# The first block of a hybrid decoder layer: x loaded by columns, ten k tiles multiplied unscaled and scaled on the way out of PSUM

## The chip, the cores and the metric

The kernel runs on one core of one Trainium2 chip. The metric is the device time of one execution in microseconds (us). The core's engines work beside each other and wait for one another through semaphores: TensorE (PE: matmuls and transposes; PEld: its weight loads), VectorE (DVE), ScalarE (ACT), GpSimd (POOL) and SyncE (SP), which here issues most of the DMAs. Each engine works through its own queue in the order in which the program left it.

## The reference, cut to what matters

One layer of two token mixers over 512 tokens of width 2048. Everything starts with an RMS norm and one wide projection:

```python
def _rmsnorm(x, w=None):
    xf = x.astype(jnp.float32)
    y = xf * lax.rsqrt(jnp.mean(xf * xf, axis=-1, keepdims=True) + NORM_EPS)
    return y if w is None else y * w.astype(jnp.float32)
...
    u = _rmsnorm(h, norm_w)
    proj = jnp.matmul(u, w_in.astype(jnp.float32))
    (ml_q, ml_k, ml_v, ml_o, ml_z, ml_i, ml_f,
     dn_qkv, dn_z, dn_b, dn_a, gate_a, gate_b) = jnp.split(proj, idx, axis=-1)
```

So u is x times a factor per token (the reciprocal root of its mean square) times a weight per column. The factor depends on all 2048 columns of a token, but it can be applied before the product with `w_in` or after it. The rest (the two mixers, the output projection, the gates, a final norm) isn't touched by the change.

## The kernel before

The kernel keeps u transposed: 16 **k tiles** of 128 columns by 512 tokens. Since a single f32r product isn't exact enough, u and every weight are split into a rounded part and a remainder (`uh`, `ul`; `wh`, `wl`), and one product becomes three matmuls: `uh` by `wh`, `ul` by `wh`, `uh` by `wl`. ScalarE makes the rounded part (`split_hi`, line 140), VectorE the remainder (`split_lo`, line 143). Weights come as tiles of two k tiles by 256 columns (`wr`, 256 KB; `load_raw`, line 172); four are in flight, and four splits of each kind.

The stage that the change touches is the start. SP issues x as eight half megabytes, two per chunk of 128 tokens (line 270). For each chunk ScalarE squares one half of the columns and VectorE the other (lines 297 and 299), the sums become the factor `rs` (lines 301 to 304, the power on GpSimd), and both engines scale the chunk in place (`scale_x`, lines 290 and 292). Then `make_u` turns each k tile: four transposes into a PSUM bank (`put`, line 313), ScalarE writes `uh` with the norm's column weight `normc` (line 314), VectorE `ul` (line 315). A tile needs all four chunks, so the first transposes wait for the factors.

The first block of the projection (`proj_cm` with `first_block` as its hook) multiplies k tile by k tile: two banks `pj` of 128 output columns each, 96 products in all. Ahead of the products of a pair, `first_block` turns tiles two further on, and from tile 8 it adds the **gate products** (lines 324 and 325): the 48 gate columns of `w_in`, kept as `wgp`, into the bank `pgr`. In the end `pgr` is copied to `gr0` and the two `pj` banks go out to memory with a scale (`spill`). The second block follows at once, over tiles 0 to 15; after its first six products TensorE turns `gr0` into the bank `pgt` (line 401), where the gate computation begins.

TensorE's order is written out by hand (`manual_schedule` for PE). The other engines' order comes from a scheduler with its own time estimates, nudged by `issue_after` and priorities. PSUM has eight banks: three `pj`, three `wk` (transposes, gates), two `o`.

## Time and profile before

| | us |
|---|---|
| median of three runs | 2155.34 (2155.28 to 2156.47) |
| the profiled execution, its own time | 2153.58 |
| its span, first to last instruction | 2151.8 |
| TensorE busy in the span | 2122.0 |
| VectorE busy | 1709.4 |
| ScalarE busy | 1042.1 |
| GpSimd busy | 431.0 |

The granted clock of TensorE is 0.999 throughout. A row of the timeline reads: start in us, how long, engine, line, operation, what is written and read (without buffer numbers), shapes, how many; in brackets the idle time of the engine before it and what ended it. A row for several instructions (x2, x8) spans from the first start to the last end. Lines in groups give the count, the busy time and the mean of one.

### The profile page before, as it was taken

How to read it: one execution, taken by the hardware profiler on the slowest of the kernel's cores; microseconds unless marked ns; L12 is line 12 of the kernel's file. 1: busy time of each engine (PE TensorE's matmuls, PEld its weight loads, DVE VectorE, ACT ScalarE, POOL GpSimd, SP SyncE). 2: the span in 40 equal slices, each digit the busy share in tenths (PEclk: the TensorE clock that was granted, in tenths of full speed). 3: DMA queues.
4: the chain of work that ended last, by engine and by line, in shares of the span. 5: the costliest groups of instructions: out<-in, count | busy, mean ns of one | idle time of the engine just before them, and what ended most of it. 6: DMA issues, size and time to landing. Idle time of an engine off the chain costs nothing. (4 is left out here: it accounts for less than half of the span.)

```text
span 2151.8 us, 31880 instructions
## 1 busy us (share of the span) xinstructions
PE 2122.0 (99%) x10544; PEld 1759.9 (82%) x10544; DVE 1709.4 (79%) x2973; ACT 1042.1 (48%) x1994; POOL 431.0 (20%) x651
## 2 busy tenths in 40 slices
PE   6999999999999999999999999999999999999998
PEld 5888888888888888888888888888888888887886
DVE  5888888788888778777756887887887878559887
ACT  5444444445444444444445545546455464345345
POOL 0000000000004000000012335334233263233211
PEclk9999999999999999999999999999999999999999
DMA  5456676667677767776767777677686677778895
GB/s 162 117 192 191 212 214 196 220 202 228 203 228 243 247 194 224 236 232 194 257 199 175 187 180 187 163 180 189 180 219 172 167 184 213 197 230 281 237 299 230
DMA packets 447143, 444.20 MB, mean 206 GB/s; under 512 B 197121, under 2 KB 303842, under 8 KB 446850
## 3 DMA queue, kind: packets, MB, share of 16 engines
q1 hardware_dynamic: 377618, 337.22, 54.5%
q0 software_dynamic: 24752, 72.90, 10.9%
q10 hardware_dynamic: 44608, 32.06, 4.7%
q8 instruction: 82, 1.34, 0.3%
q14 instruction: 83, 0.68, 0.1%
HBM read 348.66 MB, written 97.58 MB: 207 GB/s over the span
## 5 line engine op out<-in xcount | busy, mean ns | idle before, releaser
L140 ACT CAST wh<-wr 128x512 fp32r<-128x512 f32 (+1 forms) x522 | 373.9, 717 | 445.4 <-PE pj L258 239.2
L143 DVE TENSOR_TENSOR wl<-wr,wh 128x512 fp32r<-128x512 f32 (+1 forms) x522 | 438.3, 840 | 175.7 <-ACT wh L140 171.4
L257 PE MATMUL pj<-uh,wh 128*128 128x512 f32 x896 | 376.2, 420 | 0.0
L259 PE MATMUL pj<-uh,wl 128*128 128x512 f32 x896 | 351.1, 392 | 0.0
L258 PE MATMUL pj<-ul,wh 128*128 128x512 f32 x896 | 350.6, 391 | 0.0
L579 PE MATMUL ps<-wl,uh 128*128 128x512 f32 x752 | 292.6, 389 | 0.0
L578 PE MATMUL ps<-wh,uh 128*128 128x512 f32 x752 | 292.6, 389 | 0.0
L580 PE MATMUL ps<-wh,ul 128*128 128x512 f32 x752 | 292.6, 389 | 0.0
L140 ACT CAST wh<-t 128x1024 fp32r<-128x1024 f32 x120 | 126.4, 1053 | 294.0 <-PE ps L580 187.2
L578 PE MATMUL ps<-wh,suh 128*128 128x512 f32 x624 | 242.9, 389 | 0.0
L579 PE MATMUL ps<-wl,suh 128*128 128x512 f32 x624 | 242.8, 389 | 0.0
L580 PE MATMUL ps<-wh,sul 128*128 128x512 f32 x624 | 242.7, 389 | 0.0
L533 POOL DMA_DIRECT2D t_d<-ts x104 | 56.6, 544 | 922.3 <-DVE ts L520 854.1
L140 ACT CAST wh<-ts 128x512 fp32r<-128x512 f32 x240 | 148.3, 618 | 184.0 <-DVE ts L538 158.4
L143 DVE TENSOR_TENSOR wl<-t,wh 128x1024 fp32r<-128x1024 f32 x120 | 146.8, 1223 | 80.3 <-ACT wh L140 79.8
L259 PEld LDWEIGHTS pj<-uh,wl 128*128 128x128 f32 x896 | 168.4, 188 | 37.4
L257 PEld LDWEIGHTS pj<-uh,wh 128*128 128x128 f32 x896 | 169.3, 189 | 30.0
L258 PEld LDWEIGHTS pj<-ul,wh 128*128 128x128 f32 x896 | 169.4, 189 | 28.2
L143 DVE TENSOR_TENSOR wl<-ts,wh 128x512 fp32r<-128x512 f32 x240 | 164.3, 685 | 32.0 <-ACT wh L140 30.5
L580 PEld LDWEIGHTS ps<-wh,ul 128*128 128x128 f32 x752 | 141.2, 188 | 29.5
L579 PEld LDWEIGHTS ps<-wl,uh 128*128 128x128 f32 x752 | 141.2, 188 | 29.5 <-DVE wl L143 0.2
L578 PEld LDWEIGHTS ps<-wh,uh 128*128 128x128 f32 x752 | 141.2, 188 | 29.2
(334 smaller groups left out, 3760.7 us busy)
## 6 DMA issues: line engine op xcount, KB each, us to landing
wr<-in_w_in_dram SPq DMA_DIRECT2D x744, 256.0 KB, 3.6
wr<-in_w_out_dram SPq DMA_DIRECT2D x138, 256.0 KB, 4.9
t_d<-ts POOLq DMA_DIRECT2D x104, 256.0 KB, 3.7
wr<-t_d SPq DMA_DIRECT2D x104, 256.0 KB, 3.9
xt<-in_x_dram SPq DMA_DIRECT2D x8, 512.0 KB, 6.3
tg_d<-X ACTq DMA_DIRECT2D x16, 256.0 KB, 6.4
tg_d<-to ACTq DMA_DIRECT2D x16, 256.0 KB, 4.7
v<-v_d SPq DMA_DIRECT2D x8, 512.0 KB, 5.8
```

Of the source, the lines that this page charges most:

```text
L140: newest["A"] = A.copy(hi, src).ins
L143: newest["V"] = V.tensor_tensor(out=lo, in0=src, in1=hi.bitcast(F32), op=ALU.subtract).ins
L257: T.matmul(ps[j], hi[:, k, wsl], uh[:, kt, :], start=(kt == 0), stop=False)
L258: T.matmul(ps[j], hi[:, k, wsl], ul[:, kt, :], start=False, stop=False)
L259: T.matmul(ps[j], lo[:, k, wsl], uh[:, kt, :], start=False, stop=(kt == KT - 1))
L533: queue.dma_start(t2_d[b % 2, i], ts[:, 0, :])
L578: T.matmul(ps[t], ah, hi, start=(g == "A" and i == 0), stop=False, skip_group_check=True)
L579: T.matmul(ps[t], ah, lo, start=False, stop=False, skip_group_check=True)
L580: T.matmul(ps[t], al, hi, start=False, stop=(i == KH - 1), skip_group_check=True)
```

## The change

It takes apart the order "all factors first, then u". In the words of the code:

- x is one tile `xt` of four chunks by 2048 columns, loaded in five pieces by columns (256, 256, 512, 256, 768), the norm's weights ahead of them and four weight tiles between them.
- k tiles 0 to 9 (`KU = 10`) are turned and split **unscaled** (with `normc` alone). From tile 4 on, ScalarE first writes the whole value into columns of `xt` that are done with, and the split is made from there (`split_u`).
- The squares for the factors are spread over steps 0 to 7 (`square`, a step is six products), the sums come at step 7 (`token_factors`).
- Tiles 10 to 15 are scaled by `rs` ahead of their transposes (`scale_x`), as before.
- Products of tiles 0 to 9 stay in banks of their own (`rawp`, and `rawg` for the gates); tiles 10 to 15 go into other banks. `factor_row` and `turn_row` make `rrow`, the factor along the free axis on all partitions, by four matmuls of a matrix of ones with diagonals of `rs`. On copying out, the raw banks are multiplied by `rrow` and the other banks are added.
- Later blocks want scaled tiles: `rescale` and `rescaled` multiply tiles 0 to 9 by `rrow`, two at a time, and split them anew. The second block takes its k tiles in the order 10 to 15, 0 to 9 (`KS`).
- ScalarE and VectorE keep the written order in this stage (`manual_schedule` for both).

```diff
-GLAG = 8
+KU = 10
...
+    KS = {q: list(range(0, KT, KP)) for q in QK}
+    KS[QK[1]] = list(range(KU, KT, KP)) + list(range(0, KU, KP))
+    plan = [("i", (ML_Q, ML_K)[a] + b * NB, k) for a, b in QK for k in KS[a, b]]
...
+    load_norms(p0, psw)
+    xt = p0.tile([P, NC, D], F32, tag="x", name="xt")
+    XC = [0, 256, 512, 1024, 1280, D]
+    for n in range(len(XC) - 1):
+        o = slice(XC[n], XC[n + 1])
+        with behind("S") if n else ExitStack():
+            newest["S"] = nc.sync.dma_start(xt[:, :, o], xv[:, :, o]).ins
+        if n in (0, 1, 3, 4):
+            with behind("S"):
+                load_raw()
...
+    def turn_row(diag):
+        pr = psw.tile([P, S], F32, tag="wk", name="prow")
+        for c in range(NC):
+            T.matmul(pr[:, c * P:(c + 1) * P], ones, diag[:, c, :], start=True, stop=True)
+        A.copy(rrow, pr)
...
+    def split_u(kt, pt):
+        hi, lo = uh[:, kt, :], ul[:, kt, :]
+        if kt < 4 or kt >= KU:
+            A.activation(hi, pt, AF.Copy, scale=normc[:, kt:kt + 1])
+            V.scalar_tensor_tensor(out=lo, in0=pt, scalar=normc[:, kt:kt + 1], in1=hi.bitcast(F32), op0=ALU.mult, op1=ALU.subtract)
+        else:
+            f = whole(kt - 4, 1)[:, 0]
+            A.activation(f, pt.rearrange("p (c t) -> p c t", t=P), AF.Copy, scale=normc[:, kt:kt + 1])
+            split_hi(hi.rearrange("p (c t) -> p c t", t=P), f)
+            split_lo(lo.rearrange("p (c t) -> p c t", t=P), f, hi.rearrange("p (c t) -> p c t", t=P))
+
+    def rescale(p):
+        k = slice(KP * p, KP * (p + 1))
+        hi, lo, rr = (by_chunk(t) for t in (uh[:, k, :], ul[:, k, :], rrow.unsqueeze(1).to_broadcast([P, KP, S])))
+        if p < 2:
+            f = uf[p] = by_chunk(p0.tile([P, KP, S], F32, tag="uf", name="uf", bufs=2))
+            V.tensor_tensor(out=f, in0=hi.bitcast(F32), in1=lo.bitcast(F32), op=ALU.add)
+        else:
+            f = uf[p] = whole(KP * p - 4, KP)
+        V.tensor_tensor(out=f, in0=f, in1=rr, op=ALU.mult)
+        split_hi(hi, f)
...
+    SPLITS = {1: 1, 3: 2, 5: 3, 7: 4, 9: 5, 11: 6, 12: 7, 13: 8, 14: 9, 15: 10}
+
+    def hook(n):
+        if n in SPLITS:
+            split_next()
...
+        if n == 7:
+            square(A, 2, 2)
+            square(V, 2, 3)
+            token_factors()
+        if n == 8:
+            split_hi(wgh, wg)
+            split_lo(wgl, wg, wgh)
+            for kt in range(4):
+                gate_products(kt)
+            scale_x(KU, KU + 2)
+            gps["diag"] = factor_row()
+        if n == 9:
+            for kt in range(4, KU):
+                gate_products(kt)
+        if n == 10:
+            turn_row(gps["diag"])
+        if n == 13:
+            turn_taps(*taps, psw)
+        if n + 2 < KT:
+            split_u(n + 2, turn_x(n + 2))
...
+        if 10 <= n < 15:
+            rescale(n - 10)
+            if n > 10:
+                rescaled(n - 11)
+            if n == 10:
+                V.tensor_tensor(out=gr0, in0=rawg[0:112, :], in1=rrow[0:112, :], op=ALU.mult)
+            if n in (11, 12):
+                V.scalar_tensor_tensor(out=qk0[n - 11], in0=rawp[n - 11], scalar=QS, in1=rrow, op0=ALU.mult, op1=ALU.mult)
+        if n == 15:
+            rescaled(4)
...
+    with tc.manual_schedule(engines={mybir.EngineType.Activation, mybir.EngineType.DVE}):
+        pts = [turn_x(kt) for kt in range(2)]
+        split_u(0, pts[0])
+        split_next()
+        split_u(1, pts[1])
+        for j, p in enumerate(first_block()):
+            V.scalar_tensor_tensor(out=qk0[j], in0=p, scalar=QS, in1=qk0[j], op0=ALU.mult, op1=ALU.add)
+            nc.scalar.dma_start(qk_d[j], qk0[j])
+        V.tensor_tensor(out=gr0, in0=gr0, in1=gps["p"][0:112, :], op=ALU.add)
...
-    ps = proj_cm(ML_Q, before=first_block)
-    for kt in range(KT - GLAG, KT):
-        gate_products(kt)
-    gr0 = wp.tile([112, S], F32, tag="tg", name="gr0", bufs=3)
-    A.copy(gr0, pgr[0:112, :])
-    spill(ps, 0, float(P) ** -0.5)
```

How this moves the queues is seen at two places. The first is VectorE at the end of the first block, up to the copy of the gate transposes (`grow<-pgt`). Before, the last steps of the block stood there so:

```order
L143 TENSOR_TENSOR wl<-wr,wh 128x512
L315 SCALAR_TENSOR_TENSOR ul<-put,normc,uh 128x512 x2
L132 TENSOR_SCALAR convc<-pprt 128x192
L133 TENSOR_SCALAR normc<-pprt 128x16
L134 TENSOR_SCALAR normc<-pprt 128x1
L143 TENSOR_TENSOR wl<-wr,wh 128x512
L315 SCALAR_TENSOR_TENSOR ul<-put,normc,uh 128x512 x2
L143 TENSOR_TENSOR wl<-wr,wh 128x512 x2
L405 COPY grow<-pgt 128x192
```

Now this is VectorE's queue from tile 12 on (`uf` and `xt` hold whole tiles, `rrow` is the factor row, `gr` and `qk` are what goes out):

```order
L357 TENSOR_TENSOR uf<-uh,ul 128x1024
L360 TENSOR_TENSOR uf<-uf,rrow 128x1024
L428 TENSOR_TENSOR gr_144<-pgr,rrow 112x512
L143 TENSOR_TENSOR wl<-wr,wh 128x512
L345 SCALAR_TENSOR_TENSOR ul<-put,normc,uh 128x512
L357 TENSOR_TENSOR uf<-uh,ul 128x1024
L360 TENSOR_TENSOR uf<-uf,rrow 128x1024
L143 TENSOR_TENSOR ul<-uf,uh 128x1024
L430 SCALAR_TENSOR_TENSOR qk_145<-pj,rrow 128x512
L143 TENSOR_TENSOR wl<-wr,wh 128x512
L345 SCALAR_TENSOR_TENSOR ul<-put,normc,uh 128x512
```

And, seven rows later on the same queue, its end:

```order
L345 SCALAR_TENSOR_TENSOR ul<-put,normc,uh 128x512
L360 TENSOR_TENSOR xt<-xt,rrow 128x2x4x128
L143 TENSOR_TENSOR ul<-xt,uh 128x1024
L143 TENSOR_TENSOR wl<-wr,wh 128x512
L360 TENSOR_TENSOR xt<-xt,rrow 128x2x4x128
L143 TENSOR_TENSOR ul<-xt,uh 128x1024
L143 TENSOR_TENSOR wl<-wr,wh 128x512
L143 TENSOR_TENSOR ul<-xt,uh 128x1024
L461 SCALAR_TENSOR_TENSOR qk_145<-pj,qk_145 128x512
L461 SCALAR_TENSOR_TENSOR qk_146<-pj,qk_146 128x512
L463 TENSOR_TENSOR gr_144<-gr_144,pgr 112x512
```

Between the tiles' own splits there are now twelve operations of 1024 columns and six of 512 that combine banks, and the last sum of the gate rows, for which `pgt` waits, is the last of them. The second place is ScalarE ahead of the gate weights `wgp`. Before:

```order
L140 CAST wh<-wr 128x512
L314 ACTIVATE uh<-put,normc 128x512 x2
L140 CAST wh<-wr 128x512
L314 ACTIVATE uh<-put,normc 128x512 x2
L140 CAST wgp<-wg 128x16x48
```

Now (`xt<-put` is the whole tile written over used columns of x, `jk,ss` a square with its sum):

```order
L348 ACTIVATE xt<-put,normc 128x4x128
L140 CAST uh<-xt 128x512
L300 ACTIVATE jk,ss<-xt 128x768
L348 ACTIVATE xt<-put,normc 128x4x128
L140 CAST uh<-xt 128x512
L140 CAST wh<-wr 128x512
L300 ACTIVATE jk,ss<-xt 128x768
L348 ACTIVATE xt<-put,normc 128x4x128
L140 CAST uh<-xt 128x512
L140 CAST wgp<-wg 128x16x48
L313 ACTIVATE xt<-xt,rs 128x256 x2
L344 ACTIVATE uh<-put,normc 128x512
```

Each tile takes two ScalarE instructions instead of one, the squares stand among them, and the cast of `wgp` comes behind all of it.

More of the change, by code (lines that the diff above doesn't have):

```diff
@@ L307, in hybrid_body @@
-    scale_x(NC - 1)
-    def make_u(kt):
-        pool, tg = ((psw, "wk"), (pso, "o"))[kt % 2]
+    jk, jv = (p0.tile([P, KP * S], F32, tag="uf", name="jk", bufs=2) for _ in range(2))
+    rawp = [psj.tile([P, S], F32, tag="pj", name="pj") for _ in range(2)]
+    rawg = psj.tile([P, S], F32, tag="pj", name="pgr")
+    gr0 = wp.tile([112, S], F32, tag="tg", name="gr0", bufs=3)
+    qk0 = [wp.tile([P, S], F32, tag="tg", name="qk0", bufs=3) for _ in range(2)]
+    uf = {}
+    QS = float(P) ** -0.5
@@ new lines, in scale_x, with factor_row @@
+    def scale_x(a, b):
+        for c in range(NC):
+            xc = xt[:, c, a * P:b * P]
+            if c % 2:
+                V.tensor_scalar(out=xc, in0=xc, scalar1=rs[:, c:c + 1], scalar2=None, op0=ALU.mult)
+            else:
+                A.mul(xc, xc, rs[:, c:c + 1])
+    def factor_row():
+        diag = p0.tile([P, NC, P], F32, tag="diag", name="diag")
+        for c in range(NC):
+            V.tensor_scalar(out=diag[:, c, :], in0=ident, scalar1=rs[:, c:c + 1], scalar2=None, op0=ALU.mult)
+        return diag
@@ L314, in make_u @@
-        done["A"] = A.activation(uh[:, kt, :], pt, AF.Copy, scale=normc[:, kt:kt + 1]).ins
-        done["V"] = V.scalar_tensor_tensor(out=ul[:, kt, :], in0=pt, scalar=normc[:, kt:kt + 1],
-                                           in1=uh[:, kt, :].bitcast(F32), op0=ALU.mult, op1=ALU.subtract).ins
-    UA = 2
-    for kt in range(UA):
-        make_u(kt)
-    pgr = psw.tile([P, S], F32, tag="wk", name="pgr")
-    def gate_products(kt):
-        T.matmul(pgr[0:112, :], wgp[:, kt, :], uh[:, kt, :], start=(kt == 0), stop=False, skip_group_check=True)
-        T.matmul(pgr[0:48, :], wgh[:, kt, :], ul[:, kt, :], start=False, stop=(kt == KT - 1), skip_group_check=True)
```

151 lines of the change are left out of this document (88 added, 63 removed).

## The prediction

> **What bounds the kernel now.** The profile's page comes first: the busy time of each engine, and TensorE's share in 40 slices of 53.8 us.
>
> ```profile
> PE 2122.0 (99%) x10544; PEld 1759.9 (82%) x10544; DVE 1709.4 (79%) x2973; ACT 1042.1 (48%) x1994; POOL 431.0 (20%) x651
> PE   6999999999999999999999999999999999999998
> ```
>
> TensorE is short of work in the first slice alone. Next I cut the program at the first product (20.70 us) and at the gate transposes of the second block (58.4 us) in the view of busy time by stretch.
>
> ```profile
> 0.00:20.70 20.70, 4.04 (x18) 3.34 (x18) 10.55 (x24) 12.61 (x18) 3.27 (x14) 1.00 0.87 278
> 20.70:35.50 14.80, 14.80 (x74) 12.41 (x73) 10.40 (x16) 8.36 (x14) 0.00 (x0) 1.00 0.45 126
> 35.50:58.40 22.90, 22.90 (x115) 17.53 (x114) 8.38 (x14) 8.45 (x14) 0.61 (x2) 1.00 0.23 59
> 20.70:2151.80 2131.10, 2117.98 (x10529) 1756.53 (x10527) 1698.86 (x2950) 1029.53 (x1977) 427.75 (x637) 1.00 0.70 206
> ```
>
> The columns are busy us of PE, PEld, DVE, ACT, POOL. Up to 20.70 TensorE worked 4.04 us. Through the first block it is busy in 37.70 of 37.70 us, VectorE in 18.8. After 20.70 it idles 13 us in all, so whatever TensorE gains or loses by 58.4 us stays nearly whole at the end. I therefore price the change at one mark: the time at which `pgt`, the transposes of the gate rows, start. Now TensorE's and VectorE's timeline:
>
> ```profile
> 0.73 1.28 ACT L297 ACT_TABLE_LOAD   x1 [0.73 <-PEq L1753]
> 4.57 1.06 ACT L297 ACTIVATE jk<-xt 128x1024 f32<-128x1024 f32 x1 [2.55 <-DMA xt<-in_x_dram]
> 4.77 0.47 SPq L106 DMA_DIRECT2D nrow<-in_norm_w_dram  x1
> 5.89 1.23 DVE L299 SCALAR_TENSOR_TENSOR jv<-xt 128x1024 f32<-128x1024 f32 x1 [5.89 <-DMA xt<-in_x_dram]
> 18.01 3.04 PE L313 MATMUL put<-ident,xt 128*128 128x128 f32 x13 [1.28 <-DVE xt L290]
> 20.70 0.78 PE L257 MATMUL pj<-uh,wh 128*128 128x512 f32 x1
> 23.31 0.39 PE L257 MATMUL pj<-uh,wh 128*128 128x512 f32 x1
> 24.45 0.39 PE L259 MATMUL pj<-uh,wl 128*128 128x512 f32 x1
> 24.68 1.03 PE L313 MATMUL put<-ident,xt 128*128 128x128 f32 x8
> 25.47 0.48 PE L257 MATMUL pj<-uh,wh 128*128 128x512 f32 x1
> 29.10 0.48 PE L257 MATMUL pj<-uh,wh 128*128 128x512 f32 x1
> 56.29 0.40 PE L325 MATMUL pgr<-ul,wgp 128*48 128x512 f32 x1
> 56.75 0.39 PE L325 MATMUL pgr<-ul,wgp 128*48 128x512 f32 x1
> 58.37 0.55 PE L401 MATMUL pgt<-ident,gr 112*128 112x112 f32 x4
> ```
>
> From these: a product starts every 0.228 us (five from 23.31 to 24.45), a transpose takes 0.10 (eight from 24.68 to 25.47), two steps together 3.63 (25.47 to 29.10), a gate product 0.23. The mark is 58.37 us.
>
> **Part 1, the early start.** Before, TensorE waited for the squares, factors and scaling of all of x. The first half megabyte had landed at 4.57 and the next 1.32 us later. Now the first piece is again half a megabyte, behind one small load whose issue took 0.47: I take 5.0 us, between 4.57 and 8 (the third half megabyte landed there, row below). The piece for the third tile stands behind 256 KB of weights: 5.0 + 0.66 + 1.32 = 7.0. Its four transposes precede the first product, which so starts at about 7.9 instead of 20.70: 12.8 us earlier. ScalarE's table load (1.28) now stands behind `normc`: the small load lands at about 3.3 (4.57 less the 1.32 that half a megabyte takes), its transpose and copy take some 0.6, the table is there at 5.3, and the first tile's transposes end at 5.8 (5.0 and four times 0.2 at the slow start): it is hidden. If TensorE never waited again, that would be the gain.
>
> **Part 2, the first eight steps.** Here the squares, done before in TensorE's idle time, stand in ScalarE's and VectorE's queues between the splits. What each issue costs, start to start:
>
> ```profile
> 8.01 1.06 ACT L297 ACTIVATE jk<-xt 128x1024 f32<-128x1024 f32 x1 [2.29 <-DMA xt<-in_x_dram]
> 8.97 0.19 ACT L297 ACTIVATION_READ_ACCUMULATOR jk<-xt 128x1 f32 x1
> 21.51 1.27 ACT L314 ACTIVATE uh<-put,normc 128x512 fp32r<-128x512 f32 x2
> 60.12 0.62 ACT L140 CAST wh<-wr 128x512 fp32r<-128x512 f32 x1
> 60.65 0.25 ACT L413 ACTIVATE sml<-sml 128x64 f32<-128x64 f32 x1
> 30.10 0.84 ACT L140 CAST wgp<-wg 128x768 fp32r<-128x768 f32 x1
> 30.99 0.95 DVE L143 TENSOR_TENSOR wgp<-wg,wgp 128x768 fp32r<-128x768 f32 x1
> L140 ACT CAST wh<-t 128x1024 fp32r<-128x1024 f32 x2 | 2.1, 1056 | 5.5 <-DVE t L519 5.5
> ```
>
> A 512-wide cast takes 0.53 (60.12 to 60.65), a copy out of PSUM on whose result the next row waits 0.69 and some 0.04 (row 21.51: 1.27 for two that overlap), a square of 768 some 0.93, scaled from 8.01 to 9.16 for 1024. The changed ScalarE queue up to `wgp`, from the first copy into `xt` on, is six copies (4.4), six casts of u (3.2), three weight casts (1.6), three squares (2.8) and `wgp` (0.84): 12.8 us. It can't begin before VectorE has squared the columns that the copy overwrites: six products at the slow start, the fourth tile's transposes, its two splits, then two squares of 512, 7.9 + 2.6 + 0.8 + 0.7 + 0.7 + 1.3, so at 14.0. One more copy waits about 1 us for VectorE's squares of the second column range. ScalarE casts `wgp` by 27.8, VectorE's part (0.95) ends at 28.5 or so. TensorE's eight steps: 7.9 + four times 3.63 + 1.1 (slow start: 20.70 to 25.47 took 4.77, not 3.63) + 1 for late splits = 24.5. The eight gate products at step 8 use `wgp`: **TensorE waits about 4 us**, and behind them stand the transposes of tile 10. That wait lies between 2 and 6, by the same counts one us either way for each engine.
>
> **Part 3, the factor row.** From 28.5: 20 gate products (4.6), 8 transposes (0.8), 12 products (2.7), four row matmuls, and the copy to `rrow` with its waits (0.8). The trace has no 128-wide f32 matmul that isn't a transpose; from a transpose to twice a product gives 0.10 to 0.46 each, and I take 0.23, the product's row. Sum 9.8: `rrow` is there at 38.3. The `diag` rows and the sums of squares run on VectorE in TensorE's shadow.
>
> By the Trainium skill's page "FP8 and Floating Point Precision", section "TensorE Precision Notes", true FP32 makes four passes; at four transposes each, an estimate of 0.4, the sum would be 0.7 us higher. No row here shows it.
>
> **Part 4, VectorE after the factor row.** This is the largest term. The changed order gives VectorE 29 rows from the first addition of `uh` and `ul` to the last sum of the gate rows: twelve 1024-wide, five weight splits, three `ul` out of PSUM, six 512-wide with PSUM, three for the taps.
>
> ```profile
> 19.50 1.40 DVE L315 SCALAR_TENSOR_TENSOR ul<-put,normc,uh 128x512 fp32r<-128x512 f32 x2
> 71.87 0.68 DVE L143 TENSOR_TENSOR wl<-wr,wh 128x512 fp32r<-128x512 f32 x1
> 72.47 1.21 DVE L373 TENSOR_TENSOR X<-uh,ul 128x1024 f32<-128x1024 f32 x1
> 73.61 0.20 DVE L428 TENSOR_SCALAR sml<-sml 128x96 f32<-128x96 f32 x1
> 45.29 0.36 DVE L132 TENSOR_SCALAR convc<-pprt 128x192 f32<-128x192 f32 x1 [2.20 <-PE pprt L131]
> L290 DVE TENSOR_SCALAR xt<-xt,rs 128x1024 f32<-128x1024 f32 x4 | 3.0, 750 | 0.7 <-POOL rs L304 0.7
> ```
>
> Start to start, 1024 wide takes 1.14 (72.47 to 73.61), a weight split 0.60 (71.87 to 72.47), `ul` 0.65 (1.40 for two of 0.75): 12 x 1.14 + 5 x 0.60 + 9 x 0.65 + 0.6 = 23.1 us. The wide rows with the repeated `rrow` aren't in the trace; 0.67 to 1.22 bound them (a tensor by a scalar: 0.75 less the 0.08 by which neighbours overlap; an addition of two, with no overlap), and I take the addition, since they too read two tensors. Three times a weight split waits for a ScalarE cast queued behind the wide cast of `uh` (1.06, the row of 1056 ns): 1.0, 0.5 and 0.5; two rows wait for their own predecessor (0.2). Ahead of all this tile 12 is still to be split after `rrow` (about 1.4). So the gate rows are complete at 38.3 + 1.4 + 23.1 + 2.2 = 65.0, and `pgt` starts at **65.3**.
>
> Over the same stretch TensorE has 42 products (9.6), 16 transposes (1.6), 12 gate products (2.8) and three small transposes (0.4): 14.4 us. It waits some 12 us, first where tile 14's transposes need the one PSUM buffer left of three (`ul` of tile 13 reads it and stands behind the rescaling), last at `pgt`. All products of the second block are queued behind `pgt`.
>
> **What costs nothing.** The second block's products are as many in either order, and its weights follow the new plan. The first block's results now go out over VectorE, in the 29 rows. The factor row and the rescaling of the last pairs are due before the second block reaches tile 0, and the mark is later. The weight loads between the pieces of x move 1 MB that was moved before 20.70 anyway (DMA share 0.87 there).
>
> **Part 5, the slow restart.** The start shows what TensorE costs after idling: 1.1 us on the first two steps (above), and 13 transposes in 2.69 (18.01 to 20.70) that take 1.3 at the later rate, together 2.5. Whether a gap of 4 to 6 us in mid-run brings this back isn't in the trace: 0 to 2.5 at the wait for `wgp`, the same at `pgt`; the wait at tile 14 would hide it. I take one, 2.5.
>
> The Trainium skill has a rule, "TensorE: Matmul & The Clock Gate", section "What's actually happening": an idle window of about 3.4 us halves the clock and a busy one restores it. By that rule both waits would restart slowly; the rows up to 23.31 agree with a slow start, and none shows a gap later.
>
> **Sum.** The mark moves from 58.37 to 65.3, +6.9, and with one restart **+9.4 us**. The profiled run took 2153.58 us (2151.8 of span and 1.8 around it), so 2163.0 by its own time; against the median of the runs, 2155.34, that is 2164.7.
>
> **The rivals.**
> - *Two restarts*: +11.9, 2167.2. For it: TensorE had worked only 4.04 us when the slow start showed; against: no row measures a gap after that.
> - *x lands late*: the pieces have runs of 1 KB instead of 4. If the first lands at 8, where row 8.01 shows the third half megabyte, everything up to `rrow` moves 3 us: +12.4, 2167.7.
> - *No wait at step 8*: ScalarE gets `wgp` through in time because its squares overlap better. Four us less and no restart: +2.9, 2158.2, no measurable change.
> - *TensorE keeps the pace, faster*: VectorE's rows after `rrow` hide behind TensorE's 14.4 us. Then `pgt` starts at 38.3 + 14.4 = 52.7, that is -5.7 us, 2149.6. It decides at 16 us of VectorE between `rrow` and the last gate sum (0.2% faster). Even with all twelve wide rows at 0.67 the 23.1 are still 17.5.
>
> **How the numbers follow.** A measurement of this kernel tells about 0.2% (4.3 us) from no change. Forecast 0.59 (2160 to 2169 by itself, the waits one us either way and the matmuls' bounds), two restarts 0.20, late x 0.06, no wait 0.09, faster 0.06. So slower 0.85, same 0.09, faster 0.06. The range, 2157.5 to 2172, takes in all but the faster case and the tails.
>
> **What would show it.** First product at 7.5 to 9 us; `wgp` split at about 28.5 with TensorE idle some 4 us before the first gate product; `rrow` at about 38; VectorE over 90% busy from 40 to 65; idle time before `put` waiting for `ul`, and 5 to 6 us before `pgt`, which starts near 65 or, after a slow restart, 67; products 0.43 apart just after either gap if it restarts. I am wrong if VectorE has idle time between 40 and 65, or if TensorE reaches `pgt` before 60.

## The result, and the profile after

The changed kernel takes **2166.69 us**, median of 4 runs (2165.01 to 2167.47), beside 2155.45 for the kernel before on the same chip: a ratio of **1.0051** with a 95% interval of 1.0039 to 1.0064. It is slower by half a per cent. The prediction was 2164.7 us, with a range of 2157.5 to 2172.

First the page's busy times and TensorE's share in 40 slices, after:

```profile
PE 2129.8 (99%) x10552; PEld 1763.7 (82%) x10552; DVE 1726.9 (80%) x2995; ACT 1046.1 (48%) x2005; POOL 430.7 (20%) x649
PE   7999999999999999999999999999999999999998
```

On this page the two kernels look alike; the first slice is even a little fuller. The difference shows only when the start is cut at the first product, the waits and the mark (the start of `pgt`). Busy time by stretch, the columns as before (PE, PEld, DVE, ACT, POOL, then the granted clock):

```profile
0.00:8.79 8.79, 2.98 (x13) 2.51 (x14) 1.96 (x4) 3.07 (x4) 1.21 (x11) 1.00 0.72 241
26.10:30.28 4.18, 0.03 (x2) 0.03 (x1) 4.00 (x9) 3.23 (x7) 1.37 (x1) 1.00 0.62 187
30.28:33.72 3.44, 3.44 (x9) 1.95 (x10) 1.17 (x6) 0.68 (x2) 0.00 (x0) 0.51 0.02 5
50.00:60.00 10.00, 5.95 (x21) 4.70 (x22) 10.00 (x15) 4.61 (x7) 0.00 (x0) 0.83 0.19 57
54.05:57.40 3.35, 3.35 (x11) 2.74 (x12) 3.35 (x5) 2.15 (x3) 0.00 (x0) 0.53 0.27 78
68.43:71.40 2.97, 2.97 (x10) 2.52 (x11) 2.21 (x9) 0.60 (x3) 0.00 (x0) 0.51 0.69 219
69.00:2162.10 2093.10, 2080.94 (x10341) 1727.34 (x10339) 1680.96 (x2920) 1012.20 (x1948) 427.53 (x635) 1.00 0.71 208
```

The first product comes at 8.79 instead of 20.70, a gain of 11.9 us. By the mark it is gone: TensorE stands still from 26.1 to 30.28 while VectorE and ScalarE work, is busy in 6 of the 10 us from 50 to 60 while VectorE is busy in all of them, and three times runs at half the clock (0.51, 0.53, 0.51). TensorE's timeline has each of these places, with what ended the wait in brackets:

```profile
8.03 1.12 PE L331 MATMUL put<-ident,xt 128*128 128x128 f32 x4 [0.93 <-DMA xt<-in_x_dram]
13.21 0.46 PE L448 MATMUL pj<-uh,wl 128*128 128x512 f32 x1
30.28 0.65 PE L371 MATMUL pgr<-uh,wgp 128*112 128x512 f32 x1 [4.15 <-DVE wgp L143]
30.73 0.63 PE L372 MATMUL pgr<-ul,wgp 128*48 128x512 f32 x1
40.17 1.05 PE L324 MATMUL prow<-diag,ones 128*128 128x128 f32 x8
41.06 0.60 PE L331 MATMUL put<-ident,xt 128*128 128x128 f32 x4
45.65 0.60 PE L331 MATMUL put<-ident,xt 128*128 128x128 f32 x4
54.05 0.96 PE L331 MATMUL put<-ident,xt 128*128 128x128 f32 x4 [4.18 <-DVE ul L345]
68.43 1.01 PE L516 MATMUL pgt<-ident,gr 112*128 112x112 f32 x4 [4.79 <-DVE gr L463]
```

The mark moved from 58.37 to 68.43, +10.1. The span moved from 2151.8 to 2162.1, +10.3. So the whole loss lies ahead of the mark, as the prediction assumed: behind it stand 2093.4 us before and 2093.7 after. The rows of ScalarE, VectorE and GpSimd that decide:

```profile
28.31 0.83 ACT L140 CAST wgp<-wg 128x768 fp32r<-128x768 f32 x1
29.17 0.96 DVE L143 TENSOR_TENSOR wgp<-wg,wgp 128x768 fp32r<-128x768 f32 x1
28.65 1.37 POOL L305 TENSOR_TENSOR rs<-rs,mhalf 128x4 f32<-128x4 f32 x1 [26.86 <-DVE rs L304]
41.26 0.59 ACT L325 COPY rrow<-prow 128x512 f32<-128x512 f32 x1 [1.59 <-PE prow L324]
47.25 0.69 DVE L143 TENSOR_TENSOR wl<-wr,wh 128x512 fp32r<-128x512 f32 x1 [1.03 <-ACT wh L140]
53.24 0.74 DVE L345 SCALAR_TENSOR_TENSOR ul<-put,normc,uh 128x512 fp32r<-128x512 f32 x1
53.91 1.22 DVE L360 TENSOR_TENSOR xt<-xt,rrow 128x1024 f32<-128x1024 f32 x1
55.04 1.22 DVE L143 TENSOR_TENSOR ul<-uf,uh 128x1024 fp32r<-128x1024 f32 x1
67.70 0.68 DVE L463 TENSOR_TENSOR gr<-gr,pgr 112x512 f32<-112x512 f32 x1
```

`wgp` is split at 30.1, the token factors are there at 30.0, `rrow` at 41.85, and the last gate sum ends at 68.4. Between the last two VectorE is busy in 23.8 of 26.5 us; its 1024-wide rows start 1.13 us apart (53.91, 55.04). The wait in the middle is one tile later than the prediction and the expectations below have it: tile 14's transposes, at 45.65, still found a PSUM buffer; those of tile 15, at 54.05, wait for `ul` of tile 14 (53.24), which stands behind rescaling.

### The profile page after: what moved, and what is told of

Same layout as the page of the kernel before. It is cut to its first block, busy times and chain, and to the rows that moved or that the text cites. A ratio compares the mean times of both kernels' runs of the same rounds, so it can differ in the third digit from the quotient of the medians.

```text
span 2162.1 us, 31920 instructions
## 1 busy us (share of the span) xinstructions
PE 2129.8 (99%) x10552; PEld 1763.7 (82%) x10552; DVE 1726.9 (80%) x2995; ACT 1046.1 (48%) x2005; POOL 430.7 (20%) x649
## 5 line engine op out<-in xcount | busy, mean ns | idle before, releaser
L250 PE MATMUL pj<-uh,wh 128*128 128x512 f32 x864 | 363.4, 421 | 0.0
L252 PE MATMUL pj<-uh,wl 128*128 128x512 f32 x864 | 338.5, 392 | 0.0
L251 PE MATMUL pj<-ul,wh 128*128 128x512 f32 x864 | 338.0, 391 | 0.0
L252 PEld LDWEIGHTS pj<-uh,wl 128*128 128x128 f32 x864 | 162.5, 188 | 36.0
L250 PEld LDWEIGHTS pj<-uh,wh 128*128 128x128 f32 x864 | 163.2, 189 | 28.7
L251 PEld LDWEIGHTS pj<-ul,wh 128*128 128x128 f32 x864 | 163.3, 189 | 27.0
```

The source lines that it names most:

```text
L250: T.matmul(ps[j], hi[:, k, wsl], uh[:, kt, :], start=(kt == ks[0]), stop=False)
L251: T.matmul(ps[j], hi[:, k, wsl], ul[:, kt, :], start=False, stop=False)
L252: T.matmul(ps[j], lo[:, k, wsl], uh[:, kt, :], start=False, stop=(kt == ks[-1] + KP - 1))
```

## The experiments

Each is the changed kernel with the edit shown. Ratios are to the kernel before, measured beside it on the same chip; the changed kernel's is 1.0051. The ratio's interval is 0.09 to 0.18% (2 to 4 us) to either side, so small effects are read from the traces, and each trace is one execution. The mark is comparable only where no products were put ahead of `pgt`.

| run | ratio (95%) | TensorE's waits at steps 8-10, tile 15, `pgt` | `rrow` | mark |
|---|---|---|---|---|
| changed | 1.0051 (1.0039-1.0064) | 4.15, 4.18, 4.79 | 41.85 | 68.43 |
| e1_fill | 1.0045 (1.0028-1.0063) | 0.50, 1.54, 1.16 | 40.43 | 67.02 |
| e2_twice | 1.0081 (1.0064-1.0098) | 4.15, 5.44, 8.09 | 42.71 | 74.89 |
| e3_later | 1.0033 (1.0022-1.0044) | 4.15, 4.18, none | 43.12 | 69.71, 18 products later |
| e4_behind | 1.0059 (1.0044-1.0074) | 4.15, none, none; 11.98 at `prf` | 42.51 | 56.43 |
| e5_gpsimd | 1.0066 (1.0051-1.0081) | 3.52, 4.17, 3.70 | 42.11 | 68.67 |
| e6_narrow | 1.0040 (1.0026-1.0054) | 2.49, 4.18, 4.80 | 37.11 | 63.69 |
| e7_unwritten | 1.0029 (1.0018-1.0041) | 2.26 (step 6), 3.20, none; 4.34 at tile 14 | 39.18 | 64.78 |
| e8_all | 1.0028 (1.0017-1.0040) | 3.49, 6.43, none | 42.17 | 69.20, 18 later |
| e9_moved | 1.0000 (0.9991-1.0009) | 4.14, 1.14, none | 41.92 | 64.97, 30 later |
| e10_moved_fill | 0.9986 (0.9977-0.9995) | 0.54, 1.14, none | 40.30 | 63.35, 30 later |
| e11_work | 1.0037 (1.0025-1.0050) | 0.75, 4.18, 4.36 | 39.51 | 66.09 |
| e12_both | 0.9985 (0.9976-0.9994) | 0.76, 1.15, none | 38.37 | 61.36, 30 later |

**e1_fill: TensorE kept busy in the gaps.**

```diff
+    def fill(out, a, b, n):
+        for _ in range(n):
+            T.matmul(out, uh[:, a, 0:P], uh[:, b, 0:out.shape[1]], start=True, stop=True, skip_group_check=True)
...
+            fill(psw.tile([P, S], F32, tag="wk", name="fill"), 0, 1, 16)
             for kt in range(4):
                 gate_products(kt)
...
+        if n == 12:
+            fill(rawg, 10, 11, 16)
...
+        fill(pgt.rearrange("p c n -> p (c n)"), 14, 15, 18)
         for c in range(NC):
             T.transpose(pgt[:, c, :], gr0[:, c * P:(c + 1) * P], ident[0:112, 0:112])
```

> Throwaway products keep TensorE busy in the three places where it stood still for over 4 us: 16 ahead of the gate products of step 8, 16 ahead of tile 14's transposes, 18 ahead of `pgt`; each writes a bank that is overwritten or free, so the output is unchanged. Theory (a gap makes TensorE restart at half rate): the gate products then start 0.23 apart instead of 0.43, the eight of them take 1.8 instead of 3.4 us, so `rrow` is there at 40.2 instead of 41.85 and `pgt` starts at about 66.8 instead of 68.4; the products behind `pgt` run at 0.23 too. Time 1.5 to 3 us less than the changed kernel: 2164 to 2165. Rival (the slow stretches have another cause than the gap, or cost nothing because VectorE sets `pgt` anyway): the gate products stay at 0.43, or `pgt` stays at 68.4; time 2166 to 2168.

TensorE's timeline in this run:

```profile
30.39 0.46 PE L371 MATMUL pgr<-uh,wgp 128*112 128x512 f32 x1 [0.50 <-DVE wgp L143]
30.69 0.40 PE L372 MATMUL pgr<-ul,wgp 128*48 128x512 f32 x1
52.62 0.66 PE L331 MATMUL put<-ident,xt 128*128 128x128 f32 x4 [1.54 <-DVE ul L345]
55.95 0.63 PE L372 MATMUL pgr<-ul,wgp 128*48 128x512 f32 x1
67.02 0.60 PE L524 MATMUL pgt<-ident,gr 112*128 112x112 f32 x4 [1.16 <-DVE gr L470]
```

The gate products run at 0.23 and the mark comes at 67.02, 0.2 from the expected 66.8. The products behind `pgt` run at 0.23 too. So two of the slow stretches follow from the standstill, and the one at `wgp` passes its 1.4 us on to the mark. The middle one stayed: the fill stands ahead of tile 14, one tile too early, tile 15 still waits 1.54, and behind that the products are 0.43 apart up to 56.8 (55.52, 55.95). Of the gains 0.9 us reach the end of the span (2161.2): behind the mark TensorE waited 3.8 us in all, the changed kernel 2.6. The time, 0.06% below the changed kernel, can't be told from it.

**e2_twice: five more VectorE rows.**

```diff
-        split_lo(by_chunk(ul[:, k, :]), uf[p], by_chunk(uh[:, k, :]))
+        for _ in range(2):
+            split_lo(by_chunk(ul[:, k, :]), uf[p], by_chunk(uh[:, k, :]))
```

> The last step of the rescaling (the 1024-wide subtraction that makes `ul`) is done twice for each of the five pairs, which changes no value: five more VectorE rows between `rrow` and the last gate sum. Theory (VectorE's row of work sets `pgt`): each costs 1.14, so `pgt` starts 5.7 us later, at about 74.1, and the time is 5.5 to 6.5 us above the changed kernel, 2172 to 2173. Rival (ScalarE's casts, or the PSUM buffers, hold the sums, and VectorE has room): `pgt` moves by less than 2 us, time 2167 to 2169.

```profile
31.17 0.74 PE L372 MATMUL pgr<-uh,wgp 128*112 128x512 f32 x1 [4.15 <-DVE wgp L143]
74.89 1.01 PE L517 MATMUL pgt<-ident,gr 112*128 112x112 f32 x4 [8.09 <-DVE gr L464]
```

On TensorE's timeline the mark is 6.5 later than in the changed kernel, of which 0.9 were there at the gate products (x landed later), so 5.6 are from five rows of 1.14. The ratio rose by 0.30%, 6.5 us. VectorE had no room: its row of work sets the mark, one for one. (This execution's span is 9.1 us longer, 2.6 of it behind the mark, where TensorE waited 4.6 us instead of 2.6.)

**e3_later: the gate work four ticks later.**

```diff
-    start(gates())
+    start(gates(), 4)
```

> The gate work starts four ticks later: 18 products of the second block stand ahead of `pgt` instead of behind it, and `pri` and all that follows keep their distance from `pgt`. TensorE then has 4.1 us of work in the place where it waited 4.79. Theory (the gate rows only have to come late enough for TensorE not to stop): the wait before `pgt` shrinks to 0.7, too short for a slow restart, `pgt` starts at 68.4 as now, and the time falls by 4 to 5.6 us, to 2161 to 2162.7. Rival (VectorE's whole load is the bound): the gate rows' chain on VectorE is late for the transposes `prf` and `prg`, a wait of some 4 us comes back there, and the time stays at 2165 to 2167.

```profile
30.31:35.97 5.66, 5.66 (x15) 3.88 (x16) 1.50 (x7) 1.73 (x4) 0.00 (x0) 0.50 0.01 3
69.71 0.61 PE L516 MATMUL pgt<-ident,gr 112*128 112x112 f32 x4
```

The first row is the stretch behind the wait for `wgp`, the second `pgt`. `pgt` waits for nothing, and `prf` doesn't either. The ratio fell by 0.18%, 3.9 us, just under the lower end expected. In the profiled execution (2162.81 us; the median is 2161.26) the half-rate stretch behind `wgp`, with a clock of 0.50, lasted 5.66 us instead of 3.44, and `rrow` came 1.3 later; whether it did so in the other runs isn't known.

**e4_behind: all rescaling behind the gate sum.**

```diff
         if 10 <= n < 15:
-            rescale(n - 10)
-            if n > 10:
-                rescaled(n - 11)
...
-        if n == 15:
-            rescaled(4)
...
         V.tensor_tensor(out=gr0, in0=gr0, in1=gps["p"][0:112, :], op=ALU.add)
+        for p in range(5):
+            rescale(p)
+            if p:
+                rescaled(p - 1)
+            if p == 1:
+                split_next()
+        rescaled(4)
```

> All rescaling (twelve 1024-wide rows, 13.7 us of VectorE) moves behind the last sum of the gate rows. VectorE then has 26.6 - 13.7 - 2 (the waits for weight casts queued behind the wide casts) = 11 us between `rrow` and that sum, less than TensorE's 14.4, so both theories expect `pgt` without a wait at 56 to 57.5 and no wait at tile 14. Theory A (the place of the rescaling is the fault): the waits of 4.18, 4.79 and 1.0 go and at least one slow restart, time 2154 to 2156.5, as before the change. Theory B (VectorE must do the rescaling and the gate rows' chain ahead of `prf` in any order): a wait of 8 to 13 us comes in the second block, at tile 0 or at the transposes `prf`/`prg`, and the time stays at 2163 to 2168.

```profile
56.43 0.55 PE L518 MATMUL pgt<-ident,gr 112*128 112x112 f32 x4
96.79 0.38 PE L561 MATMUL prf<-ident,sml 128*8 128x128 f32 x1 [11.98 <-DVE sml L548]
```

The mark is at 56.43 without a wait, 2 us *earlier* than in the kernel before, and the time no better (1.0059). The 12 us came back whole at `prf`, whose input is the end of the gate rows' chain on VectorE. Theory B holds: an early `pgt` is worth nothing while VectorE still owes the same work ahead of `prf`.

**e5_gpsimd: `wgp` early.**

```diff
         if n == 5:
             square(V, 1, 2)
+            G.tensor_copy(wgh, wg)
+        if n == 6:
+            split_lo(wgl, wg, wgh)
...
-            split_hi(wgh, wg)
-            split_lo(wgl, wg, wgh)
             for kt in range(4):
```

> The gate weights are split early: GpSimd casts them at step 5 and VectorE subtracts at step 6, instead of ScalarE and VectorE at step 8. Theory A (the place of `wgp` in ScalarE's queue alone holds TensorE at step 8): the wait of 4.15 goes and the slow restart behind it (1.6), everything from `rrow` to `pgt` comes 5.7 us earlier, `pgt` at 62.7, time about 2161, a ratio of 1.0025 to the kernel before. Theory B (the token factors are as late as `wgp`): in the changed kernel `rs` was there at 30.0 and tile 10's columns were scaled by 31.0, so TensorE does the eight gate products at 26 to 28 and then waits some 3 us for that scaling ahead of tile 10's transposes, which start at 31 to 32 instead of 33.7; a gap of 3 may or may not restart slowly. `pgt` at 66 to 67, time 2164 to 2166, a ratio of 1.0038 to 1.0048.

VectorE, GpSimd and TensorE in their timelines:

```profile
24.15 0.95 DVE L143 TENSOR_TENSOR wgp<-wg,wgp 128x768 fp32r<-128x768 f32 x1
30.23 1.37 POOL L305 TENSOR_TENSOR rs<-rs,mhalf 128x4 f32<-128x4 f32 x1 [8.63 <-DVE rs L304]
32.20 0.97 PE L331 MATMUL put<-ident,xt 128*128 128x128 f32 x4 [3.52 <-ACT xt L313]
```

`wgp` is ready 5 us earlier and the wait only changes its name: tile 10's transposes wait 3.52 for the columns scaled by `rs`. That is theory B's wait, but later and dearer than it said: tile 10 at 32.2 instead of 31 to 32, the mark at 68.67 instead of 66 to 67, the ratio 1.0066 instead of at most 1.0048. VectorE's subtraction now stands ahead of the last squares, and `rs` comes at 31.6 instead of 30.0. Two results of the same queues were due together; speeding one delayed the other. The ratio's interval overlaps the changed kernel's, so the two times can't be told apart.

**e6_narrow: cheaper squares.**

```diff
-        w = SQ[n].stop - SQ[n].start
-        xc, to = xt[:, c, SQ[n]], ss[:, c, n:n + 1]
+        w = 64
+        xc, to = xt[:, c, SQ[n].start:SQ[n].start + w], ss[:, c, n:n + 1]
```

> Each square takes 64 columns of its range instead of 512 or 768, so the factors come from 192 of 2048 columns: part of the sums is left out, and the output differs. Removed are about 0.65 us from each of ScalarE's four squares and 0.5 to 0.75 from each of VectorE's eight, and with them most of ScalarE's two waits (1.63 and 1.18) for columns that VectorE still squares. Theory (squares in the splits' queues make `wgp` and the factors late): `wgp` is split 1.5 to 4.8 us earlier, at 25.3 to 28.6, the wait before the gate products shrinks by as much, `pgt` comes 1.5 to 5 us earlier, time 2161 to 2165. Rival (the splits follow TensorE's transposes and the loads of x, and the squares only fill holes): `wgp` within 1 us of 30.1, time 2166 to 2167.

```profile
27.07 0.45 PE L371 MATMUL pgr<-uh,wgp 128*112 128x512 f32 x1 [2.49 <-DVE wgp L143]
```

`wgp` is 3.2 us earlier, the mark 4.7: these 3.2, and the 1.6 of the half rate, which doesn't follow the shorter wait of 2.49. The wait shrank by 1.7 only, since TensorE came to it 1.5 earlier as well. So the squares in the splits' queues make steps 8 to 10 late. The two waits behind `rrow` are what they were, 4.18 and 4.80.

**e7_unwritten: the scheduler's order.**

```diff
-    with tc.manual_schedule(engines={mybir.EngineType.Activation, mybir.EngineType.DVE}):
+    with ExitStack():
```

> ScalarE and VectorE take the scheduler's order in this stage instead of the written one; the instructions are the same. Theory (the number of VectorE's rows sets `pgt`, in any order): from `rrow` to the last gate sum VectorE still needs 25 to 27 us, `pgt` moves only as `wgp` does, and the time stays within 2 us of 2166.7. Rival (the written order itself makes `wgp` late, or puts rescaling ahead of what TensorE waits for): `wgp` or `pgt` come 3 us or more earlier, time 2160 to 2164.

VectorE and TensorE in their timelines, and the stretch after TensorE's first wait:

```profile
22.04 1.22 DVE L357 TENSOR_TENSOR uf<-uh,ul 128x1024 f32<-128x1024 f32 x1
25.66 0.95 DVE L143 TENSOR_TENSOR wgp<-wg,wgp 128x768 fp32r<-128x768 f32 x1
25.12 0.79 PE L447 MATMUL pj<-ul,wh 128*128 128x512 f32 x1 [2.26 <-DVE ul L143]
64.78 0.55 PE L516 MATMUL pgt<-ident,gr 112*128 112x112 f32 x4
25.12:28.00 2.88, 2.88 (x9) 2.38 (x10) 2.69 (x5) 0.46 (x1) 2.10 (x1) 0.50 0.62 173
```

My theory's time fell and its rival held: 2160.5 us, ratio 1.0029. The same instructions, the mark 3.7 earlier. Most of that is there at `rrow`, 2.7 us earlier (39.18): `wgp` is split at 26.6 instead of 30.1, so the written order itself made it late, and TensorE waits 2.26 at step 6 instead of 4.15 for `wgp`. From `rrow` to the last gate sum it took 25.4 us instead of 26.6, inside the theory's 25 to 27, but not for the theory's reason. The scheduler puts the additions of `uh` and `ul` at 22 and 23 us, ahead of `rrow`, which they don't need; so two rows fewer stand behind it, VectorE waits some 5 us for ScalarE and for TensorE's products ahead of the last sums, and `pgt` waits for nothing. TensorE lost its time at tiles 14 and 15 instead (4.34 and 3.20). I had held the number of VectorE's rows behind `rrow` to be fixed, and two of them weren't.

**e8_all: GpSimd takes three multiplications.** With e3's and e5's edits, and:

```diff
-        V.tensor_tensor(out=f, in0=f, in1=rr, op=ALU.mult)
+        (G if p > 1 else V).tensor_tensor(out=f, in0=f, in1=rr, op=ALU.mult)
...
-        if 10 <= n < 15:
-            rescale(n - 10)
-            if n > 10:
-                rescaled(n - 11)
+        if 10 <= n:
+            if 0 <= n - 11 < 5:
+                rescale(n - 11)
+            if 0 <= n - 12 < 5:
+                rescaled(n - 12)
...
-        if n == 15:
-            rescaled(4)
...
         V.tensor_tensor(out=gr0, in0=gr0, in1=gps["p"][0:112, :], op=ALU.add)
+        for p in range(5, 6):
+            if p < 5:
+                rescale(p)
+            if p and p >= 4:
+                rescaled(p - 1)
```

> Four edits together: GpSimd multiplies by `rrow` for tiles 4 to 9 (three of VectorE's 1.14 us rows go, 3.4 us), the rescaling stands one step later, so that tile 14's transposes find their buffer, the gate work starts four ticks later as in the run before, and the gate weights are split early. Theory (after `rrow` only VectorE's rows hold TensorE, and late gate rows no longer stop it): the waits of 4.18 and 4.79 shrink to 3 us or less together and don't restart slowly, `pgt` with 18 products ahead of it starts at 59 to 63, and the time falls to 2154 to 2158, a ratio of 0.9993 to 1.0012 to the kernel before. Rival (GpSimd's rows and VectorE's slow each other, or GpSimd, at 1.1 to 1.3 us for half the width, is itself late): VectorE's wide rows take over 1.4 us or wait for GpSimd, and the time stays above 2160.

GpSimd's and VectorE's timelines:

```profile
42.24 8.50 POOL L360 TENSOR_TENSOR xt<-xt,rrow 128x1024 f32<-128x1024 f32 x3 [10.61 <-ACT rrow L325]
45.13 0.74 DVE L345 SCALAR_TENSOR_TENSOR ul<-put,normc,uh 128x512 fp32r<-128x512 f32 x1
45.79 2.75 DVE L357 TENSOR_TENSOR uf<-uh,ul 128x1024 f32<-128x1024 f32 x1
48.58 3.24 DVE L360 TENSOR_TENSOR uf<-uf,rrow 128x1024 f32<-128x1024 f32 x1
55.97 1.23 DVE L360 TENSOR_TENSOR uf<-uf,rrow 128x1024 f32<-128x1024 f32 x1
```

The theory fell, its rival's mechanism held (the median of 2159.6 is just under the rival's 2160). While GpSimd worked (42.24 to 50.74) two of VectorE's wide rows took 2.75 and 3.24 us instead of 1.22, and a weight split 1.15 instead of 0.68; right after, 1.23 again. The three rows taken from VectorE (3.4 us) cost 4.0 us in three others, and tile 15 waited 6.43. A row that reads PSUM was not slowed in the same time (45.13: 0.74).

**e9_moved and e10_moved_fill: VectorE's work placed otherwise.** The second is the first with e1's sixteen fill products at step 8.

```diff
+    def whole_u(p):
+        k = slice(KP * p, KP * (p + 1))
+        f = uf[p] = by_chunk(p0.tile([P, KP, S], F32, tag="uf", name="uf", bufs=2))
+        V.tensor_tensor(out=f, in0=by_chunk(uh[:, k, :]).bitcast(F32), in1=by_chunk(ul[:, k, :]).bitcast(F32), op=ALU.add)
...
+        if n == 9:
+            whole_u(0)
+            whole_u(1)
...
-    start(gates())
-    start(u_sums(), 7)
+    start(gates(), 6)
+    start(u_sums(), 12)
```

`rescale` no longer makes these additions itself. The rescaling stands one step later, as in e8_all, and all of it is on VectorE; by that its last subtraction falls behind the last gate sum.

> No work is removed, VectorE's work is only placed otherwise: the two additions of `uh` and `ul` (1.14 us each) at step 9, where VectorE waits for tile 10's transposes; the rescaling one step later, so that the splits out of PSUM stand ahead of it; the gate work six ticks later (30 products, 6.9 us, ahead of `pgt`), and the sums of the later stage five ticks later, so that they don't stand ahead of the gate rows' chain. Theory (VectorE's row of work between `rrow` and the points where TensorE needs a result makes the loss): the wait at tile 14 falls from 4.18 to under 2.5, that at `pgt` from 4.79 to under 1, neither with a slow restart, no wait over 1 us at `prf`; time 2155.5 to 2158.5, a ratio to the kernel before of 1.0000 to 1.0015. Rival (VectorE lacks the time in any placing, as when all rescaling stood behind the gate sum): a wait of 3 us or more comes back at `prf` or in the second block, time above 2160, ratio over 1.0022.

> As the run beside it, and 16 throwaway products ahead of the gate products of step 8, where TensorE still waits 4.15 for `wgp`. Theory: the gate products start 0.23 apart, `rrow` and all behind it come 1.6 us earlier, the time is 1 to 2 us below the run beside it, a ratio of 0.9993 to 1.0008 to the kernel before. Rival (the restart costs nothing at the end, since VectorE and not TensorE sets `pgt`): the same time as the run beside it, within 0.7 us.

TensorE's timeline of the first, then of the second:

```profile
49.32 0.66 PE L331 MATMUL put<-ident,xt 128*128 128x128 f32 x4 [1.14 <-DVE ul L345]
64.97 0.55 PE L527 MATMUL pgt<-ident,gr 112*128 112x112 f32 x4
```

```profile
30.29 0.45 PE L375 MATMUL pgr<-uh,wgp 128*112 128x512 f32 x1 [0.54 <-DVE wgp L143]
63.35 0.55 PE L532 MATMUL pgt<-ident,gr 112*128 112x112 f32 x4
```

The mechanism is the theory's: with no row of VectorE's removed, the loss is gone (1.0000, the lower edge of what was expected), since the waits behind `rrow` fell from 10 us (1.02, 4.18, 4.79) to under 2. Three of the wide rows left the stretch from `rrow` to the last gate sum, the two additions ahead of it and the last subtraction behind it, and it took 22.9 us instead of 26.6. The edits were made together, so their shares aren't known; the later gate work alone (e3_later) took back 0.18%. Filling the gap at `wgp` takes 1.6 more off the mark; the medians differ by 3.4 us (2154.21 and 2150.77, 11 runs each) and the spans by 3.3, more than the 1 to 2 expected. Most of the rest is in shorter waits behind the mark (3.7 us in all in the first, 2.3 in the second).

**e11_work and e12_both: real work in the gap at `wgp`.** The second adds e9's edits.

```diff
             split_lo(wgl, wg, wgh)
-            for kt in range(4):
-                gate_products(kt)
             scale_x(KU, KU + 2)
...
-        if n == 9:
-            for kt in range(4, KU):
-                gate_products(kt)
...
-        if n + 2 < KT:
+        if n + 2 < KT and n not in (8, 9):
             split_u(n + 2, turn_x(n + 2))
...
+            if n == 9:
+                for kt in range(4):
+                    gate_products(kt)
+                split_u(10, turn_x(10))
+                for kt in range(4, KU):
+                    gate_products(kt)
+                split_u(11, turn_x(11))
             if j and kt0 >= KU:
```

> The changed kernel with one part in another order on TensorE: the twelve products of steps 8 and 9 stand ahead of the gate products of tiles 0 to 9 and of the transposes of tiles 10 and 11, instead of between them. They are 2.8 us of real work in the place where TensorE waited 4.15 for `wgp`. Theory (the loss up to `rrow` is the wait and the restart, and the loss behind it is VectorE's row, which starts at `rrow`): less than 1.5 us are left of the wait, the gate products run at 0.23, `rrow` comes 3.5 to 4.5 us earlier, at 37.3 to 38.4, and `pgt`, 26.6 behind it, at 64 to 65; the waits of 4.2 and 4.8 behind `rrow` stay as they are. Time 3.5 to 4.5 us below the changed kernel, a ratio of 1.0030 to 1.0036 to the kernel before, if all of it reaches the end; as the fill of the gaps showed, up to 2 us of such a gain can be lost behind `pgt` (1.0045). Rival (the factors, at 30.0, hold tile 10 and with it `rrow`): `rrow` less than 1.5 us earlier, ratio 1.0045 to 1.0051.

> The run beside it together with the placing of VectorE's work that reached the time of the kernel before (additions at step 9, rescaling one step later, gate work six ticks later, later sums five ticks later); nothing is thrown away. Theory: the two parts add, `rrow` at 37 to 38, `pgt` at 61 to 62.5, no wait over 2 us behind `rrow`, time 3 to 4.5 us below that kernel, a ratio of 0.9979 to 0.9987 to the kernel before. Rival (VectorE, now asked 3.5 us earlier, is the bound behind `rrow`): waits of 2 us or more come back at tile 14, `pgt` or `prf`, ratio 0.9992 to 1.0005.

Two stretches of e11_work, then e12_both's mark:

```profile
25.73:28.95 3.22, 1.90 (x5) 0.75 (x5) 3.04 (x8) 3.14 (x6) 0.53 (x1) 0.97 0.79 220
28.95:32.36 3.41, 3.41 (x8) 2.69 (x9) 3.06 (x9) 2.54 (x5) 0.84 (x1) 0.53 0.08 29
```

```profile
61.36 0.55 PE L529 MATMUL pgt<-ident,gr 112*128 112x112 f32 x4
```

In e11_work `rrow` came 2.3 us earlier, between the two expectations: the gap is filled, yet from 28.95 on the products ran at a clock of 0.53 (in the stretch before, TensorE was busy for 1.90 of 3.22 us, in pieces). In e12_both the same instructions (busy for 1.89 of 3.22 us, 26.05 to 29.27) were followed by the full clock, 1.00. The two parts add as expected: mark at 61.4, ratio 0.9985, only `rrow`, at 38.4, is 0.4 later than expected. This kernel and e10_moved_fill are faster than both kernels, 3 to 4 us below the one before with intervals that end below 1, and e12_both is so without throwaway work.

## Why the prediction was right, step by step

The sign, the size and the places were right: the forecast's +9.4 us was measured as +11 (1.0051), inside its own range of 2160 to 2169. Between the two profiled executions the span moved by 10.3, 0.9 more than the forecast, and part of the errors cancelled: `wgp` came 1.6 later than forecast, the way from there to `rrow` took 0.3 more besides the restart, VectorE's row 0.4 less, and the restarts 1.6 ahead of the mark and 0.2 net behind it, instead of 2.5.

One sign named ahead failed as it was written: from 40 to 65 us VectorE was busy in 20.9 of 25 us, 84% and not over 90, so it had the idle time that was to prove me wrong. The idle time is 2.0 us just ahead of `rrow`'s rows, which came 3.5 us later than forecast, and the waits of 1.0, 0.5 and 0.5 for weight casts, which part 4 had counted itself.

- **Part 1, first product at 7.9:** 8.79. The third tile's piece of x landed later than estimated (transposes at 8.03, after 0.93 of waiting). In the twelve experiments these transposes start anywhere between 7.65 and 8.93, so this term is uncertain by a good half us.
- **Part 2, `wgp` at 28.5, TensorE waiting 4:** 30.1 and 4.15. The size of the wait was right because both ends moved by 1.6: the first product by 0.9, and the first eight steps by 0.7 more. The slow start lasted to 13.21, with eight products and a tile's transposes in it, and cost 2.1 us instead of 1.1; the late splits cost 0.7 instead of 1. e6_narrow shows the named cause: cheaper squares, earlier `wgp`. What the step did not say, e5_gpsimd showed: the token factors were due at the same time (30.0), so `wgp` alone was not the bound.
- **Part 3, 9.8 us from `wgp` to `rrow`:** 11.7, of which 1.6 are the restart of part 5. Four row matmuls took 0.89 (40.17 to 41.06), 0.22 each; I had taken 0.23. The estimate of 0.4 each was wrong by its price for a pass, and not by the count. The Trainium skill's page "FP8 and Floating Point Precision", section "TensorE Precision Notes", has four passes for true FP32. I had taken a transpose (0.10) for a pass; taken from the products instead, 512 columns every 0.228 us, 128 columns are 0.057, and four times that is 0.23, which the measured 0.22 agrees with. The trace shows eight records for the four matmuls, 0.11 apart.
- **Part 4, 27.0 us of VectorE from `rrow` to `pgt`:** 26.6 (41.85 to 68.43). Wide rows with the repeated `rrow` take 1.13 to 1.14, and the wait of 1.0 for a weight cast is there (47.25). This largest term was right, though the first long wait in it came at tile 15 and not at tile 14, and e2_twice confirms that it counts one for one. Its unspoken premise, that all 29 rows must stand between `rrow` and the last gate sum, was wrong for three of them: the two additions (e7_unwritten, e9_moved) and the last subtraction (e9_moved).
- **Part 5, one restart, 2.5:** there are three, behind gaps of 4.15, 4.18 and 4.79, with granted clocks of 0.51, 0.53 and 0.51. The one in the middle is hidden, as assumed. The others cost 1.6 and 1.4, each less than the 2.5 taken from the start, together more. So the rival of two restarts (2167.2) was nearer in mechanism and in time than the forecast. The Trainium skill's page "TensorE: Matmul & The Clock Gate", section "What's actually happening", has the rule that the prediction gave for it, an idle window of about 3.4 us; these three gaps of over 4 us agree with it, and shorter ones below don't.
- **All of it reaches the end:** nearly. Of the third restart's 1.4 us, 1.2 came back in shorter waits hundreds of us later (TensorE's waits behind the mark, `pgt`'s own left out, sum to 3.8 before and 2.6 after). Other executions show the exchange with the other sign: behind the mark e2_twice took 2.6 us more than the changed kernel, e5_gpsimd 2.4. So a shift of the mark reaches the end to within some 2.6 us, and the close agreement of +10.1 and +10.3 is in part luck.
- **The other rivals:** x late and no wait at step 8 did not occur. For "TensorE keeps the pace", decided at 16 us of VectorE, e4_behind made the condition true, `pgt` at 56.4, and the gain still failed at `prf`. The condition named was not enough: VectorE's debt had to be counted up to `prf` too, and not up to `pgt` alone. Nor was it needed for a smaller gain: in e12_both VectorE took 22.9 us from `rrow` to the last gate sum, and with the gate work moved later the kernel was 3 us faster than the one before.

## What to carry to other kernels

An early start is worth only what the engine that pays for it can spare: count that engine's rows up to each point where the first engine needs one of its results, the next one too, since an unpaid row moves the wait rather than removing it. Before giving up such a trade, look for rows that stand behind a result they don't read, and for consumers that can come later; here that took the +0.5% back with the same work, and work moved into the remaining gap made it -0.15%. Where two results of one queue are due together, hastening one delays the other, so fill the gap with work that is ready.

## What the hardware showed that I had not expected

- **TensorE's clock falls without a long gap.** The changed kernel's gaps of 4.2 to 4.8 us were each followed by 3 to 3.4 us at about half the clock, in e3_later one of 4.15 by 5.7, in e5_gpsimd one of 3.52 by some 4. But so were a gap of 2.26 (e7_unwritten, clock 0.50) and one of 1.54 (e1_fill, clock 0.59 from 52.62 to 56.77), while one of 2.49 (e6_narrow) was not; and in e11_work work broken by pauses of at most 0.75 us (busy 1.90 of 3.22 us) was followed by 0.53, while the same instructions in e12_both kept the full clock. A rule by the length of one gap, such as the 3.4 us in the Trainium skill's page "TensorE: Matmul & The Clock Gate", section "HAM oscillation — how this bites in real kernels", is too lenient here. The same page's "What's actually happening" calls the window free-running, which would fit the difference between equal stretches; no run here measures the window itself.
- **VectorE's rows slow down beside GpSimd's.** In e8_all VectorE's wide rows with two inputs in SBUF took 2.75 and 3.24 us beside GpSimd's, 1.22 alone; the row with one input in PSUM kept its 0.74. GpSimd's own rows took 2.83 each, some twice the 1.11 to 1.38 that rows of half the width take in the kernel before, so whether they were slowed isn't shown. The Trainium skill's page "SBUF — State Buffer", section "Who interferes with whom", says that a VectorE instruction with two SBUF inputs contends with a GpSimd instruction that reads SBUF; this trace agrees.
- **The granted clock does not show the first slow start.** The products from 8.79 to 13.21 are 0.43 apart, like those at a clock of 0.51 later, yet the column reads 1.00 up to there. Why isn't shown by any run here; the spacing of the products is the safer reading.
